# Seven wide dummy matmuls in place of fourteen narrow ones, and a q half transposed behind the first bias slot

## The chip, the cores and the metric

The kernel runs on one core of one Trainium2 chip. The metric is the device time of one execution in microseconds (us); each version is measured as the median of several executions. The profile is one execution, and its span is about 1.8 us shorter than the metric in most executions. TensorE is PE in the profile (PEld is its weight load), VectorE is DVE, ScalarE is ACT, GpSimd is POOL, SyncE is SP.

## The reference

```python
batch, n_heads, seq_len, head_dim = 4, 8, 1024, 64      # q, k, v of that shape; bias 1 x 1 x 1024 x 1024
scores = (1 / sqrt(head_dim)) * q @ k.T + bias
attn = exp(scores - max) / (sum(exp(scores - max)) + 1e-8)
return attn @ v                                           # float32
```

There are 32 heads, worked on in 16 pairs. The kernel takes exp(scores) on ScalarE, multiplies by exp(bias) on VectorE, and divides at the end by a sum that a column of ones in v delivers.

## The kernel before

The scores go through slots of up to three banks of PSUM, where this kernel's matmuls write their results; the slots alternate in two buffers, and four of the slots in that sequence hold transposed bias instead. Only parts are shown.

```python
zeros = consts.tile([P, HQ // 2], BF)                     # P = 128, HQ = 512
...
# the start: loads, then dummies, matmuls on zeros whose results nobody reads
nc.vector.memset(zeros[:], 0.0)
...
def dummy(n):
    nc.tensor.matmul(wm[:, 0, :n], zeros[:, :P], zeros[:, :n], start=True, stop=True)
for i in range(12):
    dummy(HQ // 2)
...                                  # casts, transposes of the first q and k halves, copies
dummy(P)
dummy(P)
s_fill(0)                            # scores of the first slot
s_exp(0)                             # the first exponential
...
# a small list scheduler orders the rest by assumed times; raw_at: when k and q of a pair have landed
raw_at = {0: (5900, 11500), 1: (22200, 23500), 2: (26000, 28500)}
...
# outputs of the last pair, in the order of time; two more halves leave at the very end
if pr == NP - 1:
    nc.sync.dma_start(out=of[2 * pr + h][:, c0:c0 + QC, :], in_=oall[:, c0:c0 + QC, :])     # three times
...
q = (nc.scalar, nc.sync)[x]          # last two outputs: one on ScalarE's queue, one on SyncE's
q.dma_start(out=of[2 * NP - 1][:, QC + x * M:QC + (x + 1) * M, :], in_=oh[:])
```

The softmax here doesn't subtract the row's maximum and nothing guards it: scores larger than these inputs give would overflow.

Of the kernel before, what the change touches and what calls it, by code (L numbers as in the profile page):

```python
# [9 lines left out]
BF = mybir.dt.bfloat16  # L10
# [5 lines left out]
def kernel(  # L16
# [15 lines left out]
    nc = tc.nc  # L32
    B, H, S, D = q.shape
    P = 128
# [4 lines left out]
    HQ = S // 2  # L39
    QC = NCH // 2  # L40
# [7 lines left out]
    consts = ctx.enter_context(tc.tile_pool(name="consts", bufs=1))  # L48
# [15 lines left out]

    k0f = consts.tile([P, 2, QC, D], F32)
    q0f = [consts.tile([P, QC, D], F32, name=f"q0f{t}") for t in range(2)]
    zeros = consts.tile([P, HQ // 2], BF)

    raws = {}
    trs = {}  # L70
# [52 lines left out]
    def s_fill(g):  # L123
        if ("S", g) not in open_ps:
            open_ps[("S", g)] = ps_s.tile([P, 3, HQ], F32, tag="s", name="ps")
        ps = open_ps[("S", g)]
        for j, b in enumerate(slots[g]):
            pr, h, qh, kc = banks[b]
            qT, kT = trs[(pr, 0)], trs[(pr, 1)]
            nc.tensor.matmul(ps[:, j, :], kT[:, kc, :], qT[:, h, qh * HQ:(qh + 1) * HQ],  # L130
                             start=True, stop=b not in late_bias)
            if b in late_bias:
                nc.tensor.matmul(ps[:, j, :], ident[:], braw[:, late_bias[b], :], start=False, stop=True)
# [109 lines left out]
    with tc.manual_schedule():  # L243
# [26 lines left out]
        wm = ps_s.tile([P, 3, HQ], F32, tag="s", name="ps")  # L270
        open_ps[("S", 0)] = wm

        def dummy(n):
            nc.tensor.matmul(wm[:, 0, :n], zeros[:, :P], zeros[:, :n], start=True, stop=True)  # L274

        for i in range(12):
            dummy(HQ // 2)

        def k_trans(c0, n, tag):
            px = ps_x.tile([P, n, P], BF, tag=tag, name="px")  # L280
# [22 lines left out]
            "p b (c q) -> p (b c) q", q=P)[:, :QC, :])  # L303
        q_out(1, pq1)
        nc.scalar.copy(kr0[:, :, 2:QC, :], k0f[:, :, 2:, :])
        dummy(P)
        dummy(P)
        s_fill(0)
        s_exp(0)
        s_fill(1)  # L310
# [28 lines left out]
        x_free = {"xa": T0 - 500, "xb": T0 + 100}  # L339
        x_unit = {}  # L340
        bias_at = {(0, 0): 10900, (0, 2): 13700, (1, 0): 18600, (1, 2): 20800}
        raw_at = {0: (5900, 11500), 1: (22200, 23500), 2: (26000, 28500)}
        pieces = [(0, 0, 1)]
        for pr in range(1, NP):
            pieces += [(pr, 1, 0), (pr, 0, 0), (pr, 1, 1), (pr, 0, 1)]
# [232 lines left out]
        while len(act_end) < NO or av_next < NA or any(last_left) or dve_q:  # L578
# [12 lines left out]
            if who == 0:  # L591
                i = a[2]
# [52 lines left out]
```

## Time and profile before

| | kernel before |
|---|---|
| time, median of the first 3 executions | 249.8 us (249.74 to 250.32) |
| span of the profiled execution | 249.0 us |
| ScalarE busy | 240.1 us (96%) |
| first exponential starts | 5.71 us |
| last bias exponential starts | 25.75 us |

ScalarE is the bound: for most of the span its exponentials follow one another without a gap (busy for 214.00 of the 214.00 us from 26 to 240). The lines that show this, and the stretch at 22 to 26 us where it is late, stand in the prediction.

```profile
q8 instruction: 1, 0.02, 1.6%
...
out_dram<-oh SPq DMA_DIRECT2D x1, 64.0 KB, 2.3
```

Two issues of the same kind on the same engine take 0.33 and 1.12 us, and in the same stretch there is one packet of kind "instruction" (16 KB; the page counts 25 of them on this queue over the whole span). Such a packet is called a fetch below: I take it to bring a part of TensorE's program. That is a reading of the profiles: they call its kind "instruction", the last three here come with 515, 266 and 3 of TensorE's recorded instructions left (the last two of the changed kernel with 502 and 259), and in the runs TensorE instructions added or removed move the last of them (at 244.59 us with 6320, 234.72 with 6306, 240.12 with 6426).

### The profile page before, as it was taken

The page shows a single profiled execution, that of the slowest core. Times are in us where ns is not written, and L with a number is a line of the kernel's source. Part 1 is how long each engine was busy: PE and PEld are TensorE (multiplying, and loading weights), DVE is VectorE, ACT ScalarE, POOL GpSimd, SP SyncE. Part 2 cuts the span into 40 slices and gives each one's busy share as a digit, 9 for nine tenths or more (in the row PEclk, how much of TensorE's full clock was granted, in tenths as well). Part 3 has the DMA queues.
Part 4 walks back from the last instruction along what each step waited for, and adds up shares of the span by engine and source line. Part 5 has one row for each costly group of instructions (what it writes and reads, how often), then busy time and mean ns, then how long its engine had stood idle before and what let it go on. Part 6 is the DMA issues. An engine that isn't in the chain of part 4 may idle for free.

```text
span 249.0 us, 7149 instructions
## 1 busy us (share of the span) xinstructions
PE 226.3 (91%) x3106; PEld 141.6 (57%) x3160; DVE 219.0 (88%) x381; ACT 240.1 (96%) x183; POOL 54.6 (22%) x76
## 2 busy tenths in 40 slices
PE   8768999999999999999999999999999999998892
PEld 4335656556665665665656555666555555565561
DVE  5207899999999999999999999999998999999883
ACT  5999999999999999999999999999999999999991
POOL 6654534202213501303230041416000000000000
PEclk9999999999999999999999999999999999999999
DMA  5999999923925994922992049789901101020201
GB/s 118 176 199 192 202 135 197 98 84 45 147 56 100 135 81 121 90 88 29 180 133 84 5 95 118 94 124 122 131 3 42 46 23 65 3 84 3 87 32 57
DMA packets 48752, 23.80 MB, mean 96 GB/s; under 512 B 34512, under 2 KB 44624, under 8 KB 48720
## 3 DMA queue, kind: packets, MB, share of 16 engines
q0 software_dynamic: 42560, 14.42, 53.5%
q1 hardware_dynamic: 5872, 8.72, 9.7%
q8 instruction: 25, 0.41, 0.7%
q10 hardware_dynamic: 288, 0.20, 0.3%
q14 instruction: 7, 0.06, 0.1%
HBM read 29.36 MB, written 8.39 MB: 152 GB/s over the span
## 4 chain that ended last, share of the span: by engine, by line
ACT 65%; PE 18%; DVE 7%; DMA 5%; issue 2%; POOL 1%; ACTq 0%
ACT E L137 64%; PE ps L130 11%; DMA kr<-in_k_dram 5%; PE po L188 3%; DVE E L163 2%; PE px L89 2%; PE ps L274 1%; DVE E L160 1%; DVE E L157 1%; DVE oall L200 1%; DVE qT L98 1%; ACT eb L150 1%; POOL vall L81 1%; POOL btraw L321 0%; PE pb L145 0%
## 5 line engine op out<-in xcount | busy, mean ns | idle before, releaser
L137 ACT ACTIVATE E<-ps 128x1536 bf16<-128x1536 f32 (+2 forms) x172 | 230.1, 1666 | 0.7 <-PE ps L130 0.7
L130 PE MATMUL ps<-qT,kT 128*128 128x512 bf16 x458 | 134.8, 379 | 12.1 <-ACT E L137 5.6
L188 PEld LDWEIGHTS <-E 128*128 128x128 bf16 x2016 | 82.0, 98 | 40.2 <-DVE E L160 3.8
L160 DVE TENSOR_TENSOR E<-E,eb 128x2048 bf16<-128x2048 bf16 x78 | 93.9, 1216 | 5.9 <-ACT eb L150 5.7
L188 PE MATMUL po<-vall,E 128*128 128x65 bf16 x2016 | 92.7, 194 | 2.5 <-DVE E L160 1.3
L130 PEld LDWEIGHTS <-kT 128*128 128x128 bf16 x512 | 45.1, 97 | 41.6 <-issue 9.9
L163 DVE TENSOR_TENSOR E<-E,eb 128x1024 bf16<-128x1024 bf16 x92 | 61.1, 684 | 1.9 <-ACT E L137 1.4
L75 POOL DMA_DIRECT2D kr<-in_k_dram x15 | 10.5, 699 | 87.1 <-PE px L89 84.1
L81 POOL DMA_DIRECT2D vall<-in_v_dram x32 | 28.1, 883 | 4.8 <-DVE kT L317 3.5
L200 DVE TENSOR_TENSOR oall<-po,rs 128x256 f32<-128x256 f32 x63 | 26.7, 425 | 2.2
L98 DVE TENSOR_TENSOR qT<-px,mask 128x1024 bf16<-128x1024 bf16 x31 | 21.3, 688 | 6.7 <-PE px L89 6.0
L76 POOL DMA_DIRECT2D qr<-in_q_dram x15 | 10.7, 715 | 26.0 <-PE px L89 22.8
L102 DVE COPY kT<-px 128x512 bf16<-128x512 bf16 x30 | 12.6, 421 | 1.9 <-PE px L89 1.5
L198 DVE RECIPROCAL rs<-po 128x4 f32<-128x4 f32 x63 | 11.1, 177 | 2.4 <-PE po L188 2.2
L89 PE MATMUL px<-ident,kr 128*64 128x128 bf16 x240 | 12.4, 224 | 0.8 <-DMA kr<-in_k_dram 0.6
L89 PE MATMUL px<-ident,qr 128*64 128x128 bf16 x248 | 12.8, 225 | 0.1
L89 PEld LDWEIGHTS <-qr 128*64 128x64 bf16 x248 | 7.9, 109 | 8.0 <-issue 5.1
L89 PEld LDWEIGHTS <-kr 128*64 128x64 bf16 x240 | 7.7, 109 | 7.6 <-issue 4.5
L150 ACT ACTIVATE eb<-pb 128x2048 bf16<-128x2048 bf16 x4 | 7.5, 1883 | 0.4 <-PE pb L145 0.4
L145 PE MATMUL pb<-ident,btraw 128*128 128x128 bf16 x64 | 4.6, 225 | 1.2 <-ACT eb L150 1.0
L145 PEld LDWEIGHTS <-btraw 128*128 128x128 bf16 x64 | 4.4, 146 | 1.5 <-issue 1.1
L157 DVE TENSOR_TENSOR E<-E,eb 128x1024 bf16<-128x1024 bf16 (+2 forms) x7 | 4.6, 686 | 0.2 <-ACT E L137 0.2
(45 smaller groups left out, 28.2 us busy)
## 6 DMA issues: line engine op xcount, KB each, us to landing
out_dram<-oall SPq DMA_DIRECT2D x28, 256.0 KB, 2.0
vall<-in_v_dram POOLq DMA_DIRECT2D x32, 128.0 KB, 5.9
kr<-in_k_dram POOLq DMA_DIRECT2D x15, 256.0 KB, 4.5
qr<-in_q_dram POOLq DMA_DIRECT2D x15, 256.0 KB, 5.2
btraw<-in_bias_dram POOLq DMA_DIRECT2D x4, 512.0 KB, 8.5
out_dram<-oall SPq DMA_DIRECT2D x7, 128.0 KB, 3.5
k0f<-in_k_dram SPq DMA_DIRECT2D x2, 128.0 KB, 3.0
q0f<-in_q_dram ACTq DMA_DIRECT2D x1, 128.0 KB, 2.5
```

The lines of the kernel that those rows point to most:

```text
L76: nc.gpsimd.dma_start(out=qr.rearrange("p t c d -> p t (c d)"), in_=qf[pr])
L81: nc.gpsimd.dma_start(out=vall[:, 2 * pr + t, :, :D], in_=vf[pr, :, t])
L89: nc.tensor.transpose(px[t * D:(t + 1) * D, c, :], src[:, t, half * QC + c, :], ident[:])
L98: nc.vector.tensor_tensor(dst[:, :, half * HQ:(half + 1) * HQ], px.rearrange("p c q -> p (c q)").unsqueeze(1).to_broadcast([P, 2, HQ]), ma ...
L102: nc.vector.tensor_copy(dst[:, half * QC:(half + 1) * QC, :], px[:])
L130: nc.tensor.matmul(ps[:, j, :], kT[:, kc, :], qT[:, h, qh * HQ:(qh + 1) * HQ], start=True, stop=b not in late_bias)
L137: nc.scalar.activation(e_at(slots[g][0], n), open_ps.pop(("S", g))[:, :n, :], ACTF.Exp, scale=scale)
L160: nc.vector.tensor_tensor(e, e, eb[:, qh, kc:kc + 2, :].unsqueeze(2).to_broadcast([P, 2, 2, HQ]), op=ALU.mult)
L163: nc.vector.tensor_tensor(e, e, eb[:, qh, kc:kc + 1, :].to_broadcast([P, n, HQ]), op=ALU.mult)
L188: nc.tensor.matmul(acc[:, i, :], e[:, 0, i * P:(i + 1) * P], vall[:, 2 * pr + h, kc, :], start=(kc == 0 and i == 0), stop=(kc == NCH - 1), ...
L198: nc.vector.reciprocal(rs[:], acc[:, :, D:D1])
L200: nc.vector.tensor_tensor(oall[:, c0:c0 + QC, :], acc[:, :, :D], rs[:].to_broadcast([P, QC, D]), op=ALU.mult)
```

## The change

Its intent: the same dummy columns with half the instructions and a smaller tile of zeros, read four times by a broadcast; and to keep the first bias slot from standing behind a q load in TensorE's order.

```diff
-    zeros = consts.tile([P, HQ // 2], BF)
+    zeros = consts.tile([P, P], BF)
...
-            nc.tensor.matmul(wm[:, 0, :n], zeros[:, :P], zeros[:, :n], start=True, stop=True)
-        for i in range(12):
-            dummy(HQ // 2)
+            nc.tensor.matmul(wm[:, 0, :n * P], zeros[:, :P], zeros[:, :P].unsqueeze(1).to_broadcast([P, n, P]),
+                             start=True, stop=True)
+        for i in range(6):
+            dummy(QC)
...
-        dummy(P)
-        dummy(P)
+        dummy(2)
...
-        raw_at = {0: (5900, 11500), 1: (22200, 23500), 2: (26000, 28500)}
+        raw_at = {0: (5900, 12600), 1: (22200, 23500), 2: (26000, 28500)}
```

TensorE's program gets 14 instructions shorter: 6306 matmuls and weight loads instead of 6320 (the page counts 3153 weight loads instead of 3160, one for each matmul; of the matmuls themselves some records can be missing).

## The prediction

One term of the sum is gone, part 2's chance of an earlier clock, which was well below 0.05 us. The sum on the path came to 0 + 0 + 0 + 0 within about 0.05 us, with that term or without it; 0.05 us for rival C off the 249.80 us that the first three executions have as their median gave 249.75 us.

ACT's ideal or unhindered steps in it are estimates from the trace before: exponentials of 512, 1024 and 1536 columns (at 5.71, 6.55 and 23.94 us) are busy for 0.60, 1.02 and 1.45 us, so about 0.427 us for each 512 columns, and those of 1536 start 1.330 us apart when nothing holds them. That gives 0.476, 0.903 and, for 2048 columns, 1.757 us. What an early clock would do to the score fills and the first exponential is an estimate too, from the 215 and 427 ns between matmuls of 512 columns.

> **What bounds the kernel now.** I read the page first: busy shares, then the clock row, then the chain that ended last. ScalarE (ACT) is the engine to watch.
>
> ```profile
> PE 226.3 (91%) x3106; PEld 141.6 (57%) x3160; DVE 219.0 (88%) x381; ACT 240.1 (96%) x183; POOL 54.6 (22%) x76
> ...
> L137 ACT ACTIVATE E<-ps 128x1536 bf16<-128x1536 f32 (+2 forms) x172 | 230.1, 1666 | 0.7 <-PE ps L130 0.7
> ```
>
> ACT is busy for 240.1 of 249.0 us, and 230.1 of those are the exponentials. The last number of the second line is the idle time ahead of them: 0.7 us. A change that gives ACT no less work can win only ahead of the first exponential, in the few places where ACT is late, and in the tail. The diff touches only the first 14 us, so I went on to busy time by stretch and to the start of ACT's timeline.
>
> ```profile
> 26.00:240.00 214.00, 202.47 (x2843) 126.58 (x2891) 203.32 (x348) 214.00 (x160) 39.70 (x50) 1.00 0.60 88
> ```
>
> In this row the columns after the stretch's length are PE, weight loads, DVE, ACT and POOL: from 26 us on ACT is busy 214.00 of 214.00 us. So the end is, to a good approximation, the time at which ACT gets going at about 25.75 us plus a constant. Before that:
>
> ```profile
> 3.56 0.41 ACT L296 CAST kr<-k0f 128x256 bf16<-128x256 f32 x1 [0.86 <-DMA k0f<-in_k_dram]
> 4.63 0.37 ACT L301 COPY kT<-px 128x256 bf16<-128x256 bf16 x1 [0.67 <-PE px L283]
> 5.07 0.40 ACT L305 CAST kr<-k0f 128x256 bf16<-128x256 f32 x1
> 5.71 0.60 ACT L137 ACTIVATE E<-ps 128x512 bf16<-128x512 f32 x1 [0.23 <-PE ps L130]
> 6.55 1.02 ACT L137 ACTIVATE E<-ps 128x1024 bf16<-128x1024 f32 x1 [0.25 <-PE ps L130]
> ```
>
> The first exponential starts at 5.71 us, at the end of a path of loads, casts, transposes and copies. Then ACT waits 0.25 us and once more 0.21 us for scores, and after 7.8 us it runs without a wait until this:
>
> ```profile
> 22.73 0.41 PE L89 MATMUL px<-ident,kr 128*64 128x128 bf16 x8 [0.59 <-DMA kr<-in_k_dram]
> ...
> 24.08 0.41 PE L89 MATMUL px<-ident,qr 128*64 128x128 bf16 x8
> 24.25 0.87 POOL L81 DMA_DIRECT2D vall<-in_v_dram  x1 [0.37 <-DMA qr<-in_q_dram]
> ...
> 24.55 1.16 PE L145 MATMUL pb<-ident,btraw 128*128 128x128 bf16 x16
> ...
> 25.75 1.88 ACT L150 ACTIVATE eb<-pb 128x2048 bf16<-128x2048 bf16 x1 [0.36 <-PE pb L145]
> ```
>
> This is the place that decides the case. [...]The k of the next head pair lands (I read 22.69 us from the semaphore records), its transposes start at 22.73 after 0.59 us of idling; the q of that pair lands at 23.96, and its transposes start at 24.08; only then come the last sixteen bias transposes, and ACT, waiting for them, starts at 25.75. The step from the exponential before (start 23.94) to this one is 1.81 us, where the same form takes 1.33 when nothing is in its way: ACT loses **0.48 us** here, to a DMA landing. The DMA row for the first 26 us shows full engines (nine tenths in each slice) from about 8 us on, so these landings are set by bytes through the queue and not by when the first exponential ran.
>
> [...]the twelve 256-column dummies start 213 ns apart[...] and the last transposes before 5 us 107 ns apart; the clock record gives the full clock from 6.37 us, and matmuls of 512 columns are then 215 ns apart instead of 427. [...]So twelve of 256 and six of 512 columns are the same time. [...]The trace has 165 ns for 128 words of zeros and 272 for 256 words of the mask, that is 0.84 ns a word.[...]
>
> **The change, part by part.** (1) The dummies ahead of the first transposes: 12 x 256 = 3072 columns become 6 x 512 = 3072 columns. Removed: six matmuls and six weight loads, which ran beside the matmuls anyway (0.15 us each against 0.21 of spacing). Time on TensorE before: 12 x 213 = 2.56 us from 1.07, so the last column goes in at 3.60. After: 6 x 427 = 2.56 us. Difference: zero. The first transposes start at 3.74, after the cast that ends at 3.57, so the dummies do not hold them back in either.
>
> (2) The memset of zeros has 64 words instead of 128: 64 x 0.84 = 54 ns less, so the dummies start at about 1.02 instead of 1.07 and end at 3.57. For the path to the first exponential that is worth nothing, since the cast rules.[...]
>
> (3) Two of 128 columns become one of 256, at 4.80. Two times 107 ns is 213 ns either way, until 5.01; the first scores wait for a copy on ACT that ends at 5.007 and start at 5.06. Zero, with 50 ns to spare.
>
> (4) The q transposes move behind the sixteen bias transposes. In the kernel before they sit at 11.36 to 11.77 us; their data landed at 11.25. The bias transposes behind them start at 11.97, held by the PSUM slot that ACT frees at 11.92, not by them. So moving them brings the bias slot forward by nothing here: it starts at 11.97 and ends at 13.10 as before, and ACT's bias exponential at 13.13 (17 ns off its ideal step) stays. What moves back is the q half: its eight transposes would run 12.93 to 13.34, the masked copy on DVE (692 ns) 13.39 to 14.08. The next score slot needs no q half for its first matmul (start 13.31) but does for the second and third: they go at 14.13 and 14.35, and the slot is full at about 14.73, where it was 14.12. ACT wants it at 14.89 (13.13 plus a step of 1.757). It fits, with 0.15 us to spare.
>
> Sum on the path: 0 + 0 + 0 + 0 within about 0.05 us. What the move buys is shelter: today a q landing later than about 11.45 would delay the bias slot and ACT behind it; afterwards it may be as late as 12.8.
>
> **The rivals.** A: the clock is released earlier and the prologue becomes faster. [...]the first two score fills would take half the time, and the excess of ACT's first two steps (0.37 and 0.33 us over what they take unhindered) would go, with up to 0.2 us on the first start. [...]Against: columns and start are the same in both kernels, so it is no difference between them; and what is won before 22 us runs into the k and q landing at 22.7 and 24.0, where the wait merely grows. Full pass-through would give 249.0; absorbed, 249.8.
>
> B: the late q half makes a new wait of ACT at 14.9. It needs DVE or the semaphores to be 0.15 us slower than I took. Even then up to 0.48 us is absorbed at 25.75, because ACT waits there in any case. Unabsorbed it would be 250.0.
>
> C: the q landing was the hidden cost in runs without the profiler, and its delay holds up the bias slot by some tenths. For: one of the three runs before is 250.32, half a microsecond above the others, and the landing at 11.25 is just 0.2 us from mattering. Against: again the wait at 25.75 swallows it. If it were paid in full, the change would win 0.1 to 0.4: 249.4 to 249.7.
>
> D: the wider broadcast read of the zeros (the same 128 columns read four times) is slower than a plain read. If each 512-column dummy took 10% longer, the dummies would end at 3.83, hold the first transposes by 0.26 us, and again be absorbed or cost 0.26.
>
> **Range and chances.** All parts come to zero on the path, and each rival that isn't zero is below 0.7 us and is followed by a wait that swallows 0.48. Rival C makes me lean to 0.05 us below the three runs' median: 249.75. The three runs spread by 0.58 us, so 249.3 to 250.2 should hold it 8 times in 10. Two per cent would be 5 us, ten times the largest lever found: same 0.985, the rest split for a chip that behaves differently.
>
> **What would show it right or wrong.** In the changed kernel's trace: six dummies 427 ns apart, the last column in by about 3.6; first exponential at 5.7 if the clock comes after 6 us, 5.4 to 5.5 if it comes before 5; q transposes right behind the bias transposes at about 12.9; the masked copy ending near 14.1, and no ACT wait before the exponential at 14.9; last bias exponential still released by bias transposes behind the q transposes, at 25.6 to 25.9, whatever the first exponential's start. I am wrong if that last time moves along with the first exponential (then the prologue counts in full), if ACT shows a wait near 14.9 (rival B), or if the span differs while the first 26 us agree, which would mean that ACT's gapless stretch is not as rigid as I take it.

## More of the kernel before

What the prediction did not look at is the end. This is SyncE's timeline there, then the DMA queues from 243 to 247 us (queue: kind: packets, MB, share of the engines' time; the last lines are issues with their size and the time from issue to landing):

```profile
244.20 0.33 SPq L203 DMA_DIRECT2D out_dram<-oall  x1
244.83 1.12 SPq L240 DMA_DIRECT2D out_dram<-oh  x1
```

## The result, and the profile after

| | before | after |
|---|---|---|
| time, median of 6 executions each | 250.18 us (249.74 to 250.75) | 249.26 us (248.91 to 250.0) |
| ratio | | 0.9965 (95%: 0.9943 to 0.9987) |
| span of the profiled execution | 249.0 us | 247.7 us |
| last bias exponential starts | 25.75 us | 25.26 us |
| last score exponential (L137) starts | 242.33 us | 241.85 us |
| from there to the end of the span | 6.65 us | 5.86 us |

A ratio here and below is the mean time of one kernel's runs over that of the other's in the same rounds, so it is not quite the ratio of the medians quoted.

The time lies 0.04 us below the range's lower end of 249.3 us, and the class is the same. But 0.9 us is gained where the prediction worked out nothing. The two profiled executions took 250.75 us, the slowest of its six, and 249.47 us, so they lie further apart than the medians. The lower rows of the table split the two profiles' difference of 1.27 us: 0.49 us by the start of the last bias exponential, nothing in the 216.6 us from there to the last score exponential, and 0.79 us after that. The middle first: the page's line of the exponentials, and ScalarE's share of the same long stretch.

```profile
L137 ACT ACTIVATE E<-ps 128x1536 bf16<-128x1536 f32 (+2 forms) x172 | 230.1, 1666 | 1.0 <-PE ps L130 1.0
```

```profile
26.00:240.00 214.00, 205.31 (x2891) 126.62 (x2890) 203.38 (x348) 214.00 (x160) 39.67 (x50) 1.00 0.60 88
```

The exponentials take 230.1 us as before, and ScalarE is again busy for 214.00 of 214.00 us. So the prediction was right that this part is rigid. Next, TensorE around the place at which the prediction saw ScalarE held by a landing, and ScalarE's step there:

```profile
22.15 0.41 PE L89 MATMUL px<-ident,kr 128*64 128x128 bf16 x8
...
23.50 0.41 PE L89 MATMUL px<-ident,qr 128*64 128x128 bf16 x8
...
24.09 1.14 PE L145 MATMUL pb<-ident,btraw 128*128 128x128 bf16 x16
```

```profile
25.26 1.89 ACT L150 ACTIVATE eb<-pb 128x2048 bf16<-128x2048 bf16 x1
```

There is no bracket behind either transpose: TensorE did not wait for k or q here. They landed at 21.71 and 22.99 us, against 22.69 and 23.96 before. The bias transposes start at 24.09, just after ScalarE's bias exponential from the same buffer has ended (22.14 to 24.03), and ScalarE waits for nothing. Last, SyncE's end:

```profile
243.72 0.33 SPq L203 DMA_DIRECT2D out_dram<-oall  x1
244.35 0.33 SPq L240 DMA_DIRECT2D out_dram<-oh  x1
```

```profile
out_dram<-oh SPq DMA_DIRECT2D x1, 64.0 KB, 1.6
```

The second issue takes 0.33 instead of 1.12 us, and its data are out 1.6 us after the issue began instead of 2.3. The DMA view of this stretch has no instruction packet. The page has 24 of them where the one before has 25, and the last one starts at 234.72 us instead of 244.59.

### The profile page after: what moved, and what is told of

Its sections match the earlier page's. It is cut to its first block, busy times and chain, and to the rows that moved or that the text cites. A ratio compares the mean times of both kernels' runs of the same rounds, so it can differ in the third digit from the quotient of the medians. Undisturbed runs are those within 1.5% of the kernel's fastest.

```text
span 247.7 us, 7189 instructions
## 1 busy us (share of the span) xinstructions
PE 229.4 (93%) x3153; PEld 140.9 (57%) x3153; DVE 218.8 (88%) x381; ACT 239.8 (97%) x183; POOL 54.8 (22%) x76
## 4 chain that ended last, share of the span: by engine, by line
ACT 75%; PE 12%; DVE 7%; issue 2%; DMA 2%; POOL 1%; ACTq 0%; POOLq 0%
ACT E L137 72%; PE ps L130 9%; ACT eb L150 3%; DVE E L163 2%; PE po L188 2%; DMA kr<-in_k_dram 2%; DVE E L160 1%; DVE E L157 1%; DVE oall L200 1%; PE px L89 1%; DVE qT L98 1%; DVE rs L198 0%; DVE kT L102 0%; POOL qT L260 0%; POOL qT L261 0%
## 5 line engine op out<-in xcount | busy, mean ns | idle before, releaser
L137 ACT ACTIVATE E<-ps 128x1536 bf16<-128x1536 f32 (+2 forms) x172 | 230.1, 1666 | 1.0 <-PE ps L130 1.0
L130 PE MATMUL ps<-qT,kT 128*128 128x512 bf16 x512 | 138.7, 378 | 9.8 <-ACT E L137 5.6
```

What stands on the lines that cost most here:

```text
L130: nc.tensor.matmul(ps[:, j, :], kT[:, kc, :], qT[:, h, qh * HQ:(qh + 1) * HQ], start=True, stop=b not in late_bias)
L137: nc.scalar.activation(e_at(slots[g][0], n), open_ps.pop(("S", g))[:, :n, :], ACTF.Exp, scale=scale)
```

## The experiments

Three theories were to be told apart. **T**, the tail: an instruction fetch falls on the last outputs of the kernel before, and a program that is 14 instructions shorter does not come to it. **P**, the prologue: the dummies themselves gain. **Q**: the moved q half gains. Each run was timed in five rounds, beside the kernel before on the same chip.

### The kernel before again

No edit.

> The kernel before, unchanged, against itself. Both theories: ratio 1.000 within 0.002. It gives a second profile of the kernel before. Theory T (tail fetch): the trace has again 25 instruction-fetch packets of 16 KB, the last at about 244.5 us from the start, and the last output's issue on SyncE takes about 1.1 us instead of 0.33. Theory P (prologue and loads): no such regularity; if the fetch at the end is not there again, theory T falls.

Median 250.42 us, ratio 0.9984 (0.9960 to 1.0007). The profile has 25 instruction packets again, the last at 244.11 us, and the last issue on SyncE took 1.31 us. So the late fetch is no accident of one execution. The last bias exponential started at 25.35 us with no wait in front of it: the landing that the prediction made the hinge was not the bound in this execution.

### Each part alone

```diff
 # dummies_only: the changed kernel with
-        raw_at = {0: (5900, 12600), ...
+        raw_at = {0: (5900, 11500), ...
 # qmove_only: the kernel before with
-        raw_at = {0: (5900, 11500), ...
+        raw_at = {0: (5900, 12600), ...
```

> The seven wide dummies alone, the q half where it was before. TensorE has 14 instructions fewer than before. Theory T (an instruction fetch at the very end is no longer reached): the whole gain of the change, ratio 0.996 to 0.997, 24 fetches, the last output's issue 0.33 us. Theory Q (the q half behind the bias slot brings the gain): ratio 1.000.

> The q half behind the first bias slot alone, dummies as before (TensorE instruction count as before). Theory T: ratio 1.000, within 0.0015, and the 25th fetch is there at about 244.5 us. Theory Q: ratio 0.996 to 0.998, with the last bias exponential starting earlier than 25.7 us.

> The q half behind the bias slot alone, once more, since its first profile had the 25th fetch only after the end barrier although TensorE has as many instructions as before. If the fetch's moment is fixed by the program: again at about 248.6, tail 5.85, ratio near 0.997. If it is by chance near a boundary: the fetch may be back near 244 with a tail of 6.65 to 7.0 us. Theory Q (moving q gains in the first 26 us): the last bias exponential's start would be earlier than in runs with the same clock release; theory T expects it on the same line (24.7 at a release of 4.1 us, 25.3 at 5.3 to 5.7, 25.75 at 6.4).

The dummies alone: 249.63 us, ratio 0.9961 (0.9935 to 0.9987), so the gain is there without the move. The profiled execution was the slowest of its six, and is instructive for another reason (the clock, below); its tail is short, with a last issue of 0.33 us.

The moved q half alone: 250.11 us, ratio 0.9981 (0.9958 to 1.0003), then in a second measurement 250.16 us, 0.9988 (0.9960 to 1.0016). No gain is shown. It also held a lesson: the first profile had a short tail, with the 25th fetch only at 248.65 us, behind the end of its span of 247.6 us; the second had it at 244.67 us, a last issue of 1.10 us and a tail of 6.64 us. SyncE's last issue in the first and in the second:

```profile
244.21 0.34 SPq L240 DMA_DIRECT2D out_dram<-oh  x1
```

```profile
244.92 1.10 SPq L240 DMA_DIRECT2D out_dram<-oh  x1
```

It is the same program: the tail goes with the fetch, even where nothing else was changed. Probably TensorE, with 6320 instructions, ends so close to what sets off a fetch that the fetch sometimes comes after the outputs; what sets it off, no run shows.

### The same number of instructions, put elsewhere

```diff
 # after_split7: the changed kernel, banks 120 to 126 (after_split60: banks 100 to 159)
+            if SPLIT0 <= b < SPLIT0 + 7:
+                for x in range(2):       # two matmuls of 256 columns instead of one of 512
+                    nc.tensor.matmul(ps[:, j, x * HQ // 2:(x + 1) * HQ // 2], kT[:, kc, :], ...)
+                continue
 # before_skip7: the kernel before
+            if (b, i) in SKIP:           # seven weighted-sum matmuls; wrong result on purpose
+                continue
 # one_dummy_less: the kernel before
-        dummy(P)
-        dummy(P)
+        dummy(2 * P)
```

> The changed kernel with seven score matmuls in the middle (banks 120 to 126, near 60 us) split into two halves of 256 columns each, so that TensorE has as many instructions as before; the prologue stays as changed. Theory T: the 25th fetch comes back near 244 us, the last issue takes 1.1 us, the gain of 0.8 us is lost: ratio to before 0.999 to 1.001. Theory P or Q (the gain is made in the prologue): the ratio stays at 0.996 to 0.997[...].

The changed kernel, with 14 instructions more in its middle, lost the gain: 250.20 us, ratio 0.9996 (0.9966 to 1.0025). SyncE's timeline and the instruction line of the DMA view, here from 239 to 247 us:

```profile
243.12 0.33 SPq L210 DMA_DIRECT2D out_dram<-oall  x1
243.75 1.48 SPq L247 DMA_DIRECT2D out_dram<-oh  x1
```

```profile
q8 instruction: 1, 0.02, 1.0%
```

The held issue is back, though the prologue is the changed one; its last bias exponential even was the earliest of all, at 24.67 us. By the times alone the interval, down to 0.9966, still touches the change's ratio; what speaks against P and Q as the main cause is the tail of 7.01 us behind so early a start.

> The kernel before with seven of its 2016 weighted-sum matmuls (and their weight loads) left out in the middle, so its result is wrong on purpose; TensorE has 14 instructions fewer, the prologue is untouched. Theory T (tail fetch): the gain of the change without the change: 24 fetches, last output's issue 0.33 us, 5.85 us from the last exponential's start to the end, ratio 0.996 to 0.997. Theory P (the gain comes from the dummies as such or from the q half): ratio 1.000, tail 6.65 us or more.

The mirror image: the kernel before, its prologue untouched, 14 instructions fewer in the middle. 249.90 us, ratio 0.9976 (0.9951 to 1.0000), short of the 0.996 to 0.997 expected and not clear of no gain by itself. SyncE's end:

```profile
243.72 0.33 SPq L206 DMA_DIRECT2D out_dram<-oall  x1
244.34 0.33 SPq L243 DMA_DIRECT2D out_dram<-oh  x1
```

The tail is 5.86 us, as after the change. I expected 24 fetches; there were 25, but the last at 249.22 us, behind the end of the span.

> The kernel before with the two 128-column dummies joined into one of 256 columns: the same columns, TensorE has 2 instructions fewer, all else as before. Theory T, with the boundary within the last two or three instructions (as the fetch came when three of TensorE's recorded instructions were left): the fetch no longer comes before the outputs are gone, tail 5.85 us, ratio 0.9965. If the boundary lies earlier, the fetch stays, tail 6.65 to 7.0, ratio 1.000. Theory P: 1.000.

A miss of theory T's sharper form: two instructions fewer do not suffice. 250.17 us, ratio 0.9995 (0.9969 to 1.0022), fetch at 244.34 us, last issue 1.55 us, tail 7.07 us. Nor does joining these two dummies by itself show a gain.

> The changed kernel with sixty score matmuls of the middle split in two halves, 120 TensorE instructions more. Theory T, collision with the last issue: the 25th fetch comes about 106 instructions before the end, near 241.5 us, where only an earlier output is under way, so the tail is 5.85 us again though there are 25 fetches; ratio 0.996 to 0.998[...]. If the fetch costs time by itself wherever it falls: ratio 0.999 to 1.001.

With 120 instructions more than the changed kernel, the fetch comes early, at 240.12 us, and the tail is short. SyncE's timeline again:

```profile
243.36 0.33 SPq L210 DMA_DIRECT2D out_dram<-oall  x1
243.98 0.33 SPq L247 DMA_DIRECT2D out_dram<-oh  x1
```

249.95 us, ratio 0.9979 (0.9955 to 1.0003), tail 5.86 us. The interval holds 1, so here too the profile decides and not the time. It is not the number of fetches that costs, and not fewer instructions as such: it is the fetch that runs while the last outputs are issued.

Single intervals are wide, but all runs together are clear. Each run's six executions have a mean span. It is 248.3 to 248.7 us in the six runs with 6318 or 6320 instructions (the kernel before again, both of the q move, one dummy less, 7 split, and the third output below), and 247.5 to 248.1 us in the six with 6306 or 6426 (the change twice, the dummies, 7 skipped, 60 split, and the attempt below), whichever prologue they have.

### Which issue is held

```diff
 # third_out_act: the kernel before
-                nc.sync.dma_start(
+                (nc.scalar if h == 0 and qh == 1 else nc.sync).dma_start(
```

> The kernel before with the last but one output (the one ahead of SyncE's last) issued from ScalarE's queue instead of SyncE's; TensorE as before, so the fetch near 244 us should be there in the profile. If SyncE's last issue is held because its queue's preceding output is stuck behind the fetch on one DMA engine: that issue is back at 0.33 us although the fetch is there, and the tail becomes 6.0 to 6.5 us (the stuck output still lands about 1.2 us after the fetch ends). If it is held for any other reason, as by the instruction stream itself: the issue still takes 1.1 to 1.5 us and the tail 6.6 to 7.0. Ratio 0.997 to 0.9995 in the first case, 1.000 in the second.

The output ahead of SyncE's last one was moved to ScalarE's queue. SyncE's end, then ScalarE's:

```profile
244.08 0.33 SPq L240 DMA_DIRECT2D out_dram<-oh  x1
```

```profile
243.46 0.34 ACTq L203 DMA_DIRECT2D out_dram<-oall  x1
243.85 0.52 ACT L237 ACTIVATE oh<-po,rh 128x64 f32<-128x64 f32 x2 [1.12 <-DVE rh L233]
244.40 0.89 ACTq L240 DMA_DIRECT2D out_dram<-oh  x1
```

SyncE's issue is back at 0.33 us although the fetch was there, at 243.78 us. But the hold moved to the other queue: ScalarE's last issue, now the second one of its queue, took 0.89 us instead of 0.36. In both placements the held issue is the one behind another output of its own queue that is still under way. Nor is the hold the whole cost. SyncE's output was not held, yet it was out only 2.2 us after its issue began, against 1.6 in the changed kernel:

```profile
out_dram<-oh SPq DMA_DIRECT2D x1, 64.0 KB, 2.2
```

The semaphore records say why. Each of these outputs lands in sixteen parts there. In all six profiles with a late fetch the output ahead of the last two (the one moved here) has fifteen parts in 1.7 us after its issue, and the sixteenth 0.81 to 1.26 us behind them; in the seven others that gap is 0.02 to 0.04 us. SyncE's output here has the same mark, one part 0.68 us late. So one part in sixteen of what is under way is delayed with the fetch; that it stands behind the fetch's packet on one DMA engine fits, but the traces do not name the engine. I had not expected ScalarE's to be held, and the tail of 6.75 us is longer than the 6.0 to 6.5 that I gave; ratio 1.0001 (0.9970 to 1.0031), no gain.

### The change again, and one attempt to do better

> The changed kernel once more. Theory T: no 16 KB fetch in the last 8 us, last issue on SyncE 0.33 us, tail from the last exponential's start 5.86 us, ratio 0.996 to 0.997. If the ratio of the first measurement was chance: 0.998 to 1.001. The last bias exponential's start should lie on the line of the clock release (24.7 at 4.1 us, 25.3 at 5.3 to 5.7, 25.75 at 6.4) unless q of pair 1 lands after 23.5 us, in which case 1.8 us after the landing.

249.72 us, ratio 0.9966 (0.9932 to 1.0000): the first measurement repeats, though this interval just reaches 1. Tail 5.87 us, no late fetch. This profile did have the wait that the prediction described, on ScalarE:

```profile
25.84 1.88 ACT L150 ACTIVATE eb<-pb 128x2048 bf16<-128x2048 bf16 x1 [0.38 <-PE pb L145]
```

The q of pair 1 had landed at 24.04 us, and 1.80 us later ScalarE started.

```diff
 # bias_first: the changed kernel
-        raw_at = {..., 1: (22200, 23500), ...
+        raw_at = {..., 1: (22200, 24800), ...
```

> The changed kernel with the q transposes of pair 1 scheduled behind the last sixteen bias transposes (the scheduler is told that q lands at 24.8 instead of 23.5 us; the order after that point moves a little too). My first reason (the wait for that q is a real cost): no wait of ScalarE before the last bias exponential in any run, so a gain over the changed kernel of some 0.1 to 0.2 us on average (two of ten profiles so far lost 0.6 and 1.1 us there); ratio to before 0.9955 to 0.9965. If the later q transposes bring a new wait further on: 0.997 to 0.999. Tail 5.86 us.

This should have sheltered the last bias slot from that landing. The profile had no wait there, but its q landed early (22.89 us), so the shelter was not put to the test. 249.98 us, ratio 0.9988 (0.9956 to 1.0021): no better than the change. Its executions' spans (mean 247.72 us) are as short as those of the change, but the time outside the span was 1.89 to 2.93 us, against 1.7 to 1.8 in nearly all executions of the other kernels. I have no explanation for that, and no version here beats the changed kernel.

### All profiles side by side

"Tail" is from the start of the last score exponential to the end of the span. "Late" is a fetch that begins within 5 us before the end of the span.

| profile | matmuls and weight loads | last fetch at, us | last issue on SyncE, us | tail, us |
|---|---|---|---|---|
| before | 6320 | 244.59, late | 1.12 | 6.65 |
| before again | 6320 | 244.11, late | 1.31 | 6.83 |
| q move, second | 6320 | 244.67, late | 1.10 | 6.64 |
| one dummy less | 6318 | 244.34, late | 1.55 | 7.07 |
| after, 7 split | 6320 | 243.52, late | 1.48 | 7.01 |
| third output on ScalarE | 6320 | 243.78, late | 0.89 (ScalarE) | 6.75 |
| q move, first | 6320 | 248.65, behind the end | 0.34 | 5.86 |
| before, 7 skipped | 6306 | 249.22, behind the end | 0.33 | 5.86 |
| dummies only | 6306 | 236.14 | 0.33 | 5.85 |
| after | 6306 | 234.72 | 0.33 | 5.86 |
| after, second | 6306 | 235.28 | 0.33 | 5.87 |
| after, 60 split | 6426 | 240.12 | 0.33 | 5.86 |
| after, bias first | 6306 | 249.15, behind the end | 0.33 | 5.86 |

In the six profiles with a late fetch, the held issue ended 0.37 to 0.40 us after the fetch's packet did, whether that packet took 0.96 or 1.41 us. The mean spans say the same without the profile's detail: 248.7 us in the 33 executions of the kernel before that ran beside the variants, 247.7 us in the 12 of the changed one, a difference of 1.0 us; the five profiles with SyncE held have a mean tail of 6.84 us, which is 0.98 more than 5.86.

## Why the prediction was right or wrong

**The time** came out at the edge: 249.26 us in the first measurement, 0.04 us below the range's lower end of 249.3, and 249.72 us in the second, inside it. The change is far from two per cent, as predicted. That the time falls at the edge of the range is luck: the range was wide for other reasons, and its middle, 249.75 us, rested on a working that has no gain in it. The kernel was expected to be practically level with the one before, and it is 0.9 us faster on the same chip; so a term is missing.

**The step that failed: the sum of the parts.** The prediction says "Sum on the path: 0 + 0 + 0 + 0 within about 0.05 us", and its part 1 counts the removed instructions by what they take on TensorE: "which ran beside the matmuls anyway". That is true and beside the point. What it left out are the DMA packets of kind "instruction", whose times move with the number of TensorE's instructions (the table above). 14 instructions fewer kept a 16 KB fetch away from the last outputs, worth 0.8 to 1.2 us in the profiles (tails of 6.64 to 7.07 against 5.86). after_split7 and before_skip7 show that it goes with the count and not with the prologue, and after_split60 and the two profiles of the q move that it is the collision. The missing term belongs to none of the rivals A to D, and none of the three signs of being wrong looks at the tail.

**The end as "the time at which ACT gets going at about 25.75 us plus a constant"** held for the stretch of 214 us and failed for the tail, which the prediction named in its second paragraph and then did not look into.

**The wait at 25.75 us** was read correctly in the profile, and its mechanism was seen again: with q landings at 23.96, 24.04 and 24.05 us, ScalarE started 1.79, 1.80 and 1.80 us later. But it was taken for a fixture, "whatever the first exponential's start", at 25.6 to 25.9 us. It was there in 3 of 13 profiles. In the others this exponential started between 24.67 and 26.66 us with no wait, so there nothing swallows what the prologue gains or loses. One profile could not tell a habit from an accident; and the 0.49 us that the profiled pair differs by at this point is not the change's doing, as the second profile of the change has 25.84.

**The clock** (rival A) was called no difference between the kernels, and nothing here contradicts that, but its swing was undervalued because it was thought to be absorbed. The release, from which matmuls of 512 columns are 215 ns apart instead of 427, came between 3.86 and 9.63 us. In profiles without the wait, a release at 4.06, 5.71, 6.88 and 9.63 us went with a last bias exponential at 24.67, 25.26, 25.50 and 26.66 us (no strict line: 3.86 went with 25.00). That this is what spreads the executions of one kernel over a microsecond is likely, but no run sets the release on purpose.

**Parts 2 and 3** were right: the zeros' memset fell from 165 to 112 ns, the dummies began at 1.00 us, 427 ns apart, the last at 3.11, so that its last column goes in at 3.54. The first exponential started at 5.69 instead of 5.71 us.

**Part 4 and rival B**: the q transposes came at 13.13 (12.93 predicted), the masked copy ended at 14.28 (14.08). Half of that is ScalarE's chain, 0.1 us later as a whole; the other half is a start behind the bias transposes that was taken 0.1 us too early. The score slot was then filled in time, and the exponential at 15.02 us followed a step of 1.774 us, 17 ns over the estimate of 1.757, with no wait. No cost, as predicted. **Rival C** did not show: moving q alone has no demonstrable gain, though an effect of a tenth or two is inside its intervals. **Rival D** was wrong: the broadcast read runs at 427 ns for 512 columns. Two sums about the rivals were wrong too: dummies ending at 3.83 would hold transposes that start at 3.74 by 0.09 us, not 0.26, and A's own parts (0.37, 0.33 and up to 0.2 us) exceed the 0.7 us that "each rival" was said to stay below.

What stays open: why the issue is held for just that long, beyond its being behind an unfinished output of its queue; why the k and q of pair 1 land up to 2.3 us apart from profile to profile; and the long time outside the span of bias_first. In the three profiles with the wait, the last of the sixteen parts of that k landed 0.8 to 1.0 us behind the fifteenth (0.01 to 0.73 us in the others), the mark that a late fetch leaves on outputs. The span's first 16 KB fetch ran at 18.3 to 18.8 us in these three, but at 18.4 to 20.1 us in the others too, so that it delays the k is argued, not shown.

## What to carry to other kernels

Look at what lies outside the engines' busy time at the very end: a DMA issue that takes three times as long as its twin (here 1.12 us against 0.33), and the instruction packets in the DMA view. A change that alters nothing but the number of instructions can move a fetch onto, or off, the last outputs (here 14 in the middle of the kernel: tails of 7.01 us with them added, 5.86 with as many left out), so before crediting a small gain to an edit, add or drop the same number of instructions somewhere harmless and see whether the gain follows the count. And a wait seen in one profile should be seen in a second one before a prediction is hung on it.
